# A decoder layer in split fp32: the odd pair of feature blocks goes to the end of the down projection as plain products

## The chip, the cores and the metric

The kernel runs on one core of a Trainium2 chip. The metric is the time of one execution on the device in microseconds. The engines are named as in the profile: PE (TensorE) multiplies matrices into PSUM, DVE (VectorE) and ACT (ScalarE) work element by element, POOL is GpSimd, SP (SyncE) issues most loads. Work from two engines on one piece of data is ordered by semaphores, and each engine executes its own instructions in program order.

## The reference

One layer of a decoder: attention in a window and gated linear attention side by side, an output projection, and a SwiGLU feed-forward part, for a prompt of 1024 tokens and 8 x 8 sample tokens. The change lies in the last product of the feed-forward part:

```python
def swiglu(h, w_gate, w_up, w_down):
    u = jax.nn.silu(jnp.einsum('btd,df->btf', h, w_gate)) * jnp.einsum('btd,df->btf', h, w_up)
    return jnp.einsum('btf,fd->btd', u, w_down)
...
x = x + swiglu(rms_norm(x, norm2[l]), w_gate[l], w_up[l], w_down[l])
```

Here d is 1024 and f is 2816, that is 22 blocks of 128 features. All of it is fp32.

## The kernel before

**Numbers in two halves.** A matrix in fp32 is kept as a rounded part hi and a remainder lo. `split_into` makes both: ACT casts hi (L1230), DVE subtracts to get lo (L1231). A product is three matmuls, hi by hi, hi by lo and lo by hi (`mm3`, L105 to L107), each 128 x 128 by 128 x 512. The sample tokens take two matmuls (`mm2`, L111, L112).

**Seven products instead of eight.** Tokens go in pairs of 128-token tiles (tp = 0 to 3), features in pairs of 128-feature blocks (p = 0 to 10, so NP is 11) and output columns in two halves of 512. For each tp and p there is so a 2 x 2 by 2 x 2 block product. It is done with seven products (numbers m = 1 to 7) of sums of blocks, and the four outputs are sums of the seven results. The seven sums of the left side are made once for all tokens by `tail(p)`: it multiplies the up projection by the activated gate (DVE, L1341), makes sums on POOL (L1351 to L1356), splits each (`put`, tiles named uo in a pool of three) and writes it to device memory `ud[p]` by a DMA issued on ACT's queue (L1348). The down projection reads them back (`load_u`, tiles u, on SP's queue, L1428). The seven sums of the right side come from two raw blocks of w_down (`blocks_W`: load on SP, L83; splits; POOL sums L1375 to L1378).

**The order of the down projection.** `CHUNKS` is (0,), (1, 2), (3, 4) ... (9, 10). For every chunk and tp, seven PSUM tiles (`pd`, eight banks in turn) collect one product for each pair of the chunk, so 21 matmuls in the first chunk and 42 in the others. The results are kept in SBUF as seven tiles Y[tp][m]. The first chunk copies them there, in turn by ACT (L1563) and DVE (L1561), the middle ones add on DVE (L1565). `residual(tp)` adds the residual input to three of the tiles on POOL. In the last chunk `finish` (tp 0 to 2) makes the four outputs from the seven sums while products come in, and for tp 3 `combined` makes sums before the last products and `finish_combined` adds products, in the order of ORDER. Outputs leave by DMAs on ACT's queue. `samples` runs at tp 3 of the first chunk and tp 1 of the others.

PE follows the order in which the program writes matmuls. The other engines' instructions are put in order by a scheduler when the program is built, and no table in the kernel sets it.

Of the kernel before, what the change touches and what calls it, by code (L numbers as in the profile page):

```python
# [37 lines left out]
def hymba_step(ctx: ExitStack, tc: tile.TileContext, x_prompt, x_sample, cache_k, cache_v, state_gla, meta,  # L38
# [1298 lines left out]
    def tail(p, cu, cg):  # L1337
# [11 lines left out]

        put(1, a11), put(2, a12), put(4, a22)  # L1350
# [8 lines left out]
    def blocks_W(pairs):  # L1359
# [12 lines left out]
        put(2, 3, 1)  # L1372
        for raw in raws:
            (b11, b12), (b21, b22) = (halves(r) for r in raw)
            nc.gpsimd.tensor_tensor(b11, b12, b11, op=ALU.subtract)  # L1375
            nc.gpsimd.tensor_tensor(b12, b22, b12, op=ALU.subtract)
            nc.gpsimd.tensor_tensor(b22, b22, b11, op=ALU.subtract)  # L1377
            nc.gpsimd.tensor_tensor(b21, b22, b21, op=ALU.subtract)  # L1378
# [41 lines left out]
    D1, D2 = slice(0, 512), slice(512, 1024)  # L1420

# [8 lines left out]

    def load_u8(p):
# [7 lines left out]
    CHUNKS = [(0,)] + [(p, p + 1) for p in range(1, NP, 2)]  # L1439
# [37 lines left out]
    def finish(tp, x22, m, ps):  # L1477

        y = Y[tp]
        t1, t2 = 2 * tp, 2 * tp + 1  # L1480
        a = y[m]
        if m != 4:
            tt(a, a, ps, op=ALU.add)
        if m == 2:
            ts(a, a, y[1], op=ALU.add)
            nc.scalar.dma_start(yp[rows(t1), D1], a)
        elif m == 7:
            ts(x22, x22, a, op=ALU.add)
            ts(y[4], a, y[4], op=ALU.subtract)
        elif m == 6:  # L1490
            tt(a, a, y[1], op=ALU.add)
            tt(y[1], a, y[5], op=ALU.add)
            ts(x22, x22, y[1], op=ALU.add)
            nc.scalar.dma_start(yp[rows(t2), D2], x22)
            tt(y[3], y[3], y[1], op=ALU.add)
            nc.scalar.dma_start(yp[rows(t1), D2], y[3])
        elif m == 4:
            tt(a, a, ps, op=ALU.subtract)
            tt(a, a, y[6], op=ALU.add)
            nc.scalar.dma_start(yp[rows(t2), D1], a)  # L1500

    def combined(tp, x22):

        y = Y[tp]
        ts(y[2], y[2], y[1], op=ALU.add)
        tt(y[6], y[6], y[1], op=ALU.add)
        tt(y[7], y[7], y[6], op=ALU.add)
        tt(y[1], y[6], y[5], op=ALU.add)
        ts(y[4], y[7], y[4], op=ALU.subtract)
        tt(y[5], y[5], y[7], op=ALU.add)  # L1510
        ts(y[3], y[3], y[1], op=ALU.add)
        ts(y[5], y[5], x22, op=ALU.add)

    def finish_combined(tp, m, ps):
        y = Y[tp]
        t1, t2 = 2 * tp, 2 * tp + 1
        if m == 1:
            nc.scalar.copy(y[6], ps)
            tt(y[2], y[2], ps, op=ALU.add)
        elif m == 2:  # L1520
            tt(y[2], y[2], ps, op=ALU.add)
            nc.scalar.dma_start(yp[rows(t1), D1], y[2])
        elif m == 6:
            tt(y[6], y[6], ps, op=ALU.add)
        elif m == 7:
            tt(y[7], y[6], ps, op=ALU.add)
            ts(y[5], y[5], y[7], op=ALU.add)
            ts(y[4], y[4], y[7], op=ALU.add)
        elif m == 5:
            tt(y[6], y[6], ps, op=ALU.add)  # L1530
            tt(y[5], y[5], ps, op=ALU.add)
            nc.scalar.dma_start(yp[rows(t2), D2], y[5])
            ts(y[3], y[3], y[6], op=ALU.add)
        elif m == 4:
            tt(y[4], y[4], ps, op=ALU.subtract)
            nc.scalar.dma_start(yp[rows(t2), D1], y[4])
        elif m == 3:
            tt(y[3], y[3], ps, op=ALU.add)
            nc.scalar.dma_start(yp[rows(t1), D2], y[3])

    DOWN = (1, 2, 3, 7, 5, 6, 4)
    NC = len(CHUNKS)
    for c, pairs in enumerate(CHUNKS):
        first, last = c == 0, c == NC - 1
        if c:
            W = blocks_W(pairs)
        for tp in range(4):
            U = [load_u(p, tp) for p in pairs]
            if last:
                x22 = xpool2.tile([P, 512], F32, tag="xh", name="x22")  # L1550
                nc.sync.dma_start(x22, x1_rows(2 * tp + 1)[:, D2])
                if tp == 3:
                    combined(tp, x22)
            for j, m in enumerate(ORDER if last and tp == 3 else DOWN):
                ps = pd()
                for i, (u, B) in enumerate(zip(U, W)):
                    mm3(ps, u[m], B[m], i == 0, i == len(pairs) - 1)
                a = Y[tp][m]
                if first:
                    if j % 2:  # L1560
                        nc.vector.tensor_copy(a, ps)  # L1561
                    else:
                        nc.scalar.copy(a, ps)  # L1563
                elif not last:
                    tt(a, a, ps, op=ALU.add)  # L1565
                elif tp == 3:
                    finish_combined(tp, m, ps)
                else:
                    finish(tp, x22, m, ps)
            if c - 1 == tp and not last:  # L1570
                residual(tp)
            if tp == (3 if first else 1):
                samples(pairs, first, last)
# [31 lines left out]
```

## Time and profile before

| | us |
|---|---|
| median of 3 runs (lowest, highest) | 1266.97 (1266.94, 1267.35) |
| profiled execution | 1262.91 |
| its span, first to last instruction | 1260.8 |
| PE busy | 1198.7 (95%) |
| DVE busy | 888.3 (70%) |
| ACT busy | 518.6 (41%) |
| POOL busy | 433.8 (34%) |

Times in the trace count from the start of the span. The down projection runs from about 997.5 us to the end. Engines overlap, so the busy times don't add up to the span. Matmuls are pipelined: a row of one shows 0.39 us, though the next starts 0.23 us later. In a timeline the square bracket at the end of a row is the time in which the engine was idle before it, and what ended it.

### The profile page before, as it was taken

What the parts mean: (1) busy time and instruction counts of PE and PEld (TensorE: products, weight loads), DVE (VectorE), ACT (ScalarE), POOL (GpSimd) and SP (SyncE); (2) the same over time, 40 slices, a digit from 0 to 9 for tenths busy, and PEclk for the clock granted to TensorE, in tenths of its full rate; (3) what the DMA queues carried; (4) which work ended last, traced back from release to release, by engine and by line L of the source; (5) the groups of instructions that cost most, each with busy time, mean ns of one, the idle gap of its engine ahead of it and who ended that gap; (6) DMA issues with size and microseconds to landing.
All of it is one profiled execution on the core that took longest, in us unless ns stands there. A gap on an engine that the chain in (4) does not pass through costs nothing.

```text
span 1260.8 us, 23242 instructions
## 1 busy us (share of the span) xinstructions
PE 1198.7 (95%) x9178; PEld 1062.6 (84%) x9178; DVE 888.3 (70%) x1756; ACT 518.6 (41%) x939; POOL 433.8 (34%) x371
## 2 busy tenths in 40 slices
PE   6999899999999989889999999999999879999995
PEld 6878788778867878889999999999999758888874
DVE  6746886798679767756666666666666675777687
ACT  5634665565565454434333333333333360222110
POOL 6212202131120110225443544354345442534186
PEclk9998999999999989999999999999999979999998
DMA  6723422243312554215524442544354595765555
GB/s 189 231 78 93 119 76 85 53 122 102 101 63 90 182 197 134 84 52 155 167 90 148 150 148 87 175 136 142 97 186 136 186 344 199 280 249 188 224 197 176
DMA packets 146186, 186.31 MB, mean 148 GB/s; under 512 B 15659, under 2 KB 114894, under 8 KB 146062
## 3 DMA queue, kind: packets, MB, share of 16 engines
q1 hardware_dynamic: 94862, 132.40, 32.3%
q10 hardware_dynamic: 49376, 45.56, 11.2%
q0 software_dynamic: 1840, 6.88, 1.6%
q8 instruction: 72, 1.18, 0.4%
q14 instruction: 36, 0.29, 0.1%
HBM read 133.43 MB, written 52.43 MB: 147 GB/s over the span
## 4 chain that ended last, share of the span: by engine, by line
PE 42%; issue 21%; POOL 15%; DVE 14%; ACT 4%; DMA 3%; SPq 0%; POOLq 0%; DVEq 0%; ACTq 0%
PE pd L105 4%; PE pd L106 4%; PE pd L107 4%; POOL raw_wu L1251 2%; ACT hi_wg L1230 2%; POOL raw_wg L1249 1%; PE pf L107 1%; PE gv L105 1%; PE pf L105 1%; PE pf L106 1%; POOL raw_wg L1248 1%; PE gv L107 1%; PE gv L106 1%; PE pw L105 1%; PE pw L106 1%
## 5 line engine op out<-in xcount | busy, mean ns | idle before, releaser
L105 PE MATMUL pd<-hi_wd,u 128*128 128x512 f32 x308 | 121.8, 395 | 13.9 <-ACT y L1563 13.5
L106 PE MATMUL pd<-lo_wd,u 128*128 128x512 f32 x308 | 121.7, 395 | 0.1
L107 PE MATMUL pd<-hi_wd,u 128*128 128x512 f32 x308 | 121.7, 395 | 0.0
L1565 DVE TENSOR_TENSOR y<-y,pd 128x512 f32<-128x512 f32 x112 | 74.7, 683 | 38.3 <-PE pd L107 38.2
L1231 DVE TENSOR_TENSOR uo<-u,uo 128x512 fp32r<-128x512 f32 x77 | 78.2, 1020 | 31.6 <-ACT uo L1230 30.2
L1230 ACT CAST hi_wg<-raw_wg 128x1024 fp32r<-128x1024 f32 (+1 forms) x44 | 41.3, 942 | 139.1 <-PE pf L106 66.0
L1231 DVE TENSOR_TENSOR lo_wu<-raw_wu,hi_wu 128x1024 fp32r<-128x1024 f32 (+1 forms) x44 | 49.2, 1118 | 55.4 <-ACT hi_wu L1230 55.4
L1230 ACT CAST hi_wd<-raw_wd 128x1024 fp32r<-128x1024 f32 x44 | 45.0, 1054 | 99.9 <-PE pd L107 32.2
L1230 ACT CAST uo<-u 128x512 fp32r<-128x512 f32 x77 | 46.7, 620 | 90.8 <-POOL u L1351 44.1
L105 PEld LDWEIGHTS pd<-hi_wd,u 128*128 128x128 f32 x308 | 58.6, 190 | 27.8 <-ACT y L1563 13.9
L1248 POOL TENSOR_TENSOR raw_wg<-raw_wg 128x512 f32<-128x512 f32 x11 | 18.4, 1671 | 160.6 <-DVE lo_wg L1231 135.4
L106 PEld LDWEIGHTS pd<-lo_wd,u 128*128 128x128 f32 x308 | 58.4, 190 | 13.5 <-DVE lo_wd L1231 0.8
L107 PEld LDWEIGHTS pd<-hi_wd,u 128*128 128x128 f32 x308 | 58.5, 190 | 12.7
L1231 DVE TENSOR_TENSOR lo_wg<-raw_wg,hi_wg 128x1024 fp32r<-128x1024 f32 (+1 forms) x44 | 48.9, 1113 | 27.9 <-ACT hi_wg L1230 27.9
L1231 DVE TENSOR_TENSOR lo_wd<-raw_wd,hi_wd 128x1024 fp32r<-128x1024 f32 x44 | 62.8, 1432 | 8.1 <-ACT hi_wd L1230 7.9
L1230 ACT CAST hi_wu<-raw_wu 128x1024 fp32r<-128x1024 f32 (+1 forms) x44 | 41.3, 938 | 55.4 <-POOL raw_wu L1249 28.4
L590 POOL TENSOR_SCALAR sg<-sg 128x512 f32<-128x512 f32 (+1 forms) x9 | 14.0, 1561 | 132.4 <-ACT sg L589 132.3
L106 PE MATMUL pw<-lo_wo,hThi 128*128 128x512 f32 x128 | 51.7, 404 | 4.0 <-DVE lo_wo L100 4.0
L105 PE MATMUL pw<-hi_wo,hThi 128*128 128x512 f32 x128 | 52.9, 413 | 0.3 <-DVE xr L1080 0.3
L107 PE MATMUL pw<-hi_wo,hTlo 128*128 128x512 f32 x128 | 51.3, 400 | 0.0
L1248 POOL TENSOR_TENSOR raw_wu<-raw_wu 128x512 f32<-128x512 f32 x11 | 14.2, 1293 | 89.1 <-DVE lo_wu L1231 89.1
L1377 POOL TENSOR_TENSOR raw_wd<-raw_wd 128x512 f32<-128x512 f32 x11 | 19.9, 1805 | 63.5 <-DVE lo_wd L1231 63.5
(734 smaller groups left out, 4283.0 us busy)
## 6 DMA issues: line engine op xcount, KB each, us to landing
ud<-uo ACTq DMA_DIRECT2D x77, 512.0 KB, 4.2
u<-ud SPq DMA_DIRECT2D x44, 896.0 KB, 6.5
raw_wo<-in_w_o_dram SPq DMA_DIRECT2D x24, 512.0 KB, 4.1
raw_wu<-in_w_up_dram SPq DMA_DIRECT2D x22, 512.0 KB, 4.0
raw_wg<-in_w_gate_dram SPq DMA_DIRECT2D x22, 512.0 KB, 4.3
raw_wd<-in_w_down_dram SPq DMA_DIRECT2D x22, 512.0 KB, 6.4
raw_q<-in_w_in_dram SPq DMA_DIRECT2D x12, 512.0 KB, 3.7
raw_gv<-in_w_in_dram SPq DMA_DIRECT2D x12, 512.0 KB, 3.4
```

Source lines behind the costliest of these rows:

```text
L105: nc.tensor.matmul(ps, lh, rh, start=first, stop=False)
L106: nc.tensor.matmul(ps, lh, rl, start=False, stop=False)
L107: nc.tensor.matmul(ps, ll, rh, start=False, stop=last)
L590: nc.gpsimd.tensor_scalar(s, s, 2.0 ** 60, None, op0=ALU.min)
L1230: nc.scalar.copy(hi, src)
L1231: nc.vector.tensor_tensor(lo, src, hi.bitcast(F32), op=ALU.subtract)
L1248: nc.gpsimd.tensor_tensor(a22, a21, a22, op=ALU.add)
L1249: nc.gpsimd.tensor_tensor(a21, a11, a21, op=ALU.subtract)
L1251: nc.gpsimd.tensor_tensor(a12, a12, a11, op=ALU.subtract)
L1377: nc.gpsimd.tensor_tensor(b22, b22, b11, op=ALU.subtract)
L1565: tt(a, a, ps, op=ALU.add)
```

## The change

The chunks are now (0, 1), (2, 3) ... (8, 9), all of two pairs. In the first one the weights of pair 1 are made right after those of pair 0, and for tp 0 all seven products of pair 0 stand ahead of the seven of pair 1, in seven banks. In chunk (8, 9) each tp ends with `combined(tp)`, which makes the four outputs' sums from the seven. Pair 10 comes last, as plain blocks: four outputs, two products each, added to the sums and written out. So `tail(10)` writes the four blocks themselves, without POOL sums, and `blocks_W` splits the two raw blocks without sums. Its samples run after tp 0 of this phase.

```diff
@@ tail
+        if p == NP - 1:
+            put(1, a11), put(5, a21), put(2, a12), put(4, a22)
+            return
         put(1, a11), put(2, a12), put(4, a22)
@@ blocks_W
-    def blocks_W(pairs):
+    def blocks_W(pairs, plain=False):
...
         put(1, 0, 0)
         put(2, 3, 1)
+        if plain:
+            return W
@@ loads
+    def load_plain(p, tp):
+        u = upool.tile([P, 7, 2, P], F32R, tag="u", name="u")
+        i, j = ORDER.index(5), ORDER.index(4)
+        assert ORDER[0:2] == (1, 2) and j == i + 1
+        nc.sync.dma_start(u[:, 0:2].bitcast(F32), ud[p][tp][:, 0:2])
+        nc.sync.dma_start(u[:, 2:4].bitcast(F32), ud[p][tp][:, i:i + 2])
+        return {m: (u[:, n, 0, :], u[:, n, 1, :]) for n, m in enumerate((1, 2, 5, 4))}
@@ finish, combined and finish_combined go; in their place
+    def combined(tp):
+        y = Y[tp]
+        x22 = xpool2.tile([P, 512], F32, tag="xh", name="x22")
+        nc.sync.dma_start(x22, x1_rows(2 * tp + 1)[:, D2])
         ts(y[2], y[2], y[1], op=ALU.add)
         tt(y[6], y[6], y[1], op=ALU.add)
+        ts(y[4], y[7], y[4], op=ALU.subtract)
         tt(y[7], y[7], y[6], op=ALU.add)
         tt(y[1], y[6], y[5], op=ALU.add)
+        ts(x22, x22, y[7], op=ALU.add)
         ts(y[3], y[3], y[1], op=ALU.add)
+        tt(y[4], y[4], y[6], op=ALU.add)
+        tt(y[5], y[5], x22, op=ALU.add)
@@ the loop
-    CHUNKS = [(0,)] + [(p, p + 1) for p in range(1, NP, 2)]
+    CHUNKS = [(p, p + 1) for p in range(0, NP - 1, 2)]
     for c, pairs in enumerate(CHUNKS):
+        first, last = c == 0, c == len(CHUNKS) - 1
+        W = W + blocks_W((1,)) if first else blocks_W(pairs)
         for tp in range(4):
             U = [load_u(p, tp) for p in pairs]
+            if first and tp == 0:
+                pss = {m: pd() for m in ORDER}
+                for i, (u, B) in enumerate(zip(U, W)):
+                    for m in DOWN:
+                        mm3(pss[m], u[m], B[m], i == 0, i == 1)
+            for j, m in enumerate(DOWN):
+                if first and tp == 0:
+                    ps = pss[m]
+                else:
+                    ps = pd()
+                    for i, (u, B) in enumerate(zip(U, W)):
+                        mm3(ps, u[m], B[m], i == 0, i == 1)
+                a = Y[tp][m]
+                if not first:
+                    tt(a, a, ps, op=ALU.add)
+                elif j % 2:
+                    nc.vector.tensor_copy(a, ps)
+                else:
+                    nc.scalar.copy(a, ps)
+            if (c, tp) in ((1, 0), (2, 1), (3, 2), (3, 3)):
+                residual(tp)
             if last:
+                combined(tp)
+            if tp == (2 if first else 1):
+                samples(pairs, first, False)
+    W = blocks_W((NP - 1,), True)
+    for tp in range(4):
+        u, y = load_plain(NP - 1, tp), Y[tp]
+        B = W[0]
+        for c, (a1, a2), (b1, b2) in ((2, (1, 2), (1, 2)), (4, (5, 4), (1, 2)), (3, (1, 2), (0, 3)), (5, (5, 4), (0, 3))):
+            ps = pd()
+            mm3(ps, u[a1], B[b1], True, False)
+            mm3(ps, u[a2], B[b2], False, True)
+            tt(y[c], y[c], ps, op=ALU.add)
+            nc.scalar.dma_start(yp[rows(2 * tp + (c > 3)), D2 if c in (3, 5) else D1], y[c])
+        if tp == 0:
+            samples((NP - 1,), False, True)
```

**ScalarE at the start of the down projection.** Of the kernel before, from the fifth of the tail's seven operand casts (uo_11451) to the first copy out of PSUM. Tiles uo are the tail's operands on their way to memory, ud10 is that memory; hi_wd_11691 and the two like it are weights of the next chunk.

```order
L1230 CAST uo_11451<-u12_11214 128x4x128
L1230 CAST hi_wd_11691<-raw_wd_11683 128x1024
L1348 DMA ud10_6155<-uo_11446 128x4x256
L1348 DMA ud10_6155<-uo_11451 128x4x256
L1230 CAST uo_11456<-u11_11213 128x4x128
L1230 CAST uo_11460<-u21_11215 128x4x128
L1348 DMA ud10_6155<-uo_11456 128x4x256
L1348 DMA ud10_6155<-uo_11460 128x4x256
L1230 CAST u8hl_11668<-u8_11666 128x2x64
L1230 CAST hi_wd_11695<-raw_wd_11687 128x1024
L1230 CAST hi_wd_11699<-raw_wd_11685 128x1024
L1563 COPY y0_1_11504<-pd_11520 128x512
```

Of the changed kernel, from the last weight cast of pair 0 (hi_wd_11420) to the first copy. The weights 11506, 11510 and 11518 are those of pair 1.

```order
L1230 CAST hi_wd_11420<-raw_wd_11402 128x1024
L1230 CAST hi_wd_11506<-raw_wd_11502 128x1024
L1342 DMA usd10_6166<-u12_11214 128x32
L1230 CAST uo_11436<-u12_11214 128x4x128
L1230 CAST uo_11440<-u21_11215 128x4x128
L1230 CAST uo_11444<-u22_11216 128x4x128
L1348 DMA ud10_6155<-uo_11436 128x4x256
L1348 DMA ud10_6155<-uo_11440 128x4x256
L1348 DMA ud10_6155<-uo_11444 128x4x256
L1230 CAST hi_wd_11510<-raw_wd_11504 128x1024
L1230 CAST hi_wd_11518<-raw_wd_11502 128x1024
L1531 COPY y0_1_11488<-pd_11530 128x512
```

Before, the first copy (L1563) stands behind all seven operand casts, their writes and three weight casts of the next chunk. Now its counterpart (L1531) stands behind four operand casts (uo_11432, the first, is further up), their writes and three casts of weights of pair 1; the fourth of these, hi_wd_11522, is the row after it. The first cast for pair 1 has moved ahead of three operand casts, and the second is behind the three writes.

**TensorE at its eighth and ninth products.** Of the kernel before, the last product of tp 0 and the first two of tp 1; the numbers tell banks (pd), weights and operands apart.

```order
L105 MATMUL pd_11550<-hi_wd_11420,u_11518 128x512
L106 MATMUL pd_11550<-lo_wd_11421,u_11518 128x512
L107 MATMUL pd_11550<-hi_wd_11420,u_11518 128x512
L105 MATMUL pd_11557<-hi_wd_11404,u_11555 128x512
L106 MATMUL pd_11557<-lo_wd_11405,u_11555 128x512
L107 MATMUL pd_11557<-hi_wd_11404,u_11555 128x512
L105 MATMUL pd_11562<-hi_wd_11408,u_11555 128x512
L106 MATMUL pd_11562<-lo_wd_11409,u_11555 128x512
L107 MATMUL pd_11562<-hi_wd_11408,u_11555 128x512
```

Of the changed kernel, the same places.

```order
L105 MATMUL pd_11535<-hi_wd_11420,u_11526 128x512
L106 MATMUL pd_11535<-lo_wd_11421,u_11526 128x512
L107 MATMUL pd_11535<-hi_wd_11420,u_11526 128x512
L105 MATMUL pd_11530<-hi_wd_11506,u_11528 128x512
L106 MATMUL pd_11530<-lo_wd_11507,u_11528 128x512
L107 MATMUL pd_11530<-hi_wd_11506,u_11528 128x512
L105 MATMUL pd_11531<-hi_wd_11510,u_11528 128x512
L106 MATMUL pd_11531<-lo_wd_11511,u_11528 128x512
L107 MATMUL pd_11531<-hi_wd_11510,u_11528 128x512
```

Before, the eighth product takes a new bank, weights that are there, and the operands of tp 1 (u_11555). Now it goes on in the first bank (pd_11530), with weights and operands (u_11528) of pair 1.

**VectorE at the end of the program.** Of the kernel before, from the last four sums of `finish` on; L1519 to L1538 are sums of the last tile out of PSUM.

```order
L1498 TENSOR_TENSOR y_4_11502<-y_4_11502,pd 128x512
L1492 TENSOR_TENSOR y_1_11497<-y_6_11499,y_5_11501 128x512
L1499 TENSOR_TENSOR y_4_11502<-y_4_11502,y_6_11499 128x512
L1495 TENSOR_TENSOR y_3_11503<-y_3_11503,y_1_11497 128x512
L1519 TENSOR_TENSOR y_2_11491<-y_2_11491,pd 128x512
L1521 TENSOR_TENSOR y_2_11491<-y_2_11491,pd 128x512
L1524 TENSOR_TENSOR y_6_11492<-y_6_11492,pd 128x512
L1526 TENSOR_TENSOR y_7_11493<-y_6_11492,pd 128x512
L1530 TENSOR_TENSOR y_6_11492<-y_6_11492,pd 128x512
L1531 TENSOR_TENSOR y_5_11494<-y_5_11494,pd 128x512
L1535 TENSOR_TENSOR y_4_11495<-y_4_11495,pd 128x512
L1538 TENSOR_TENSOR y_3_11496<-y_3_11496,pd 128x512
```

Of the changed kernel, from the first SBUF sum of `combined` for tp 3 on; L1548 adds the plain products.

```order
L1498 TENSOR_TENSOR y_6_11476<-y_6_11476,y_1_11474 128x512
L1527 TENSOR_TENSOR y_4_11479<-y_4_11479,pd 128x512
L1501 TENSOR_TENSOR y_1_11474<-y_6_11476,y_5_11478 128x512
L1500 TENSOR_TENSOR y_7_11477<-y_7_11477,y_6_11476 128x512
L1504 TENSOR_TENSOR y_4_11479<-y_4_11479,y_6_11476 128x512
L1548 TENSOR_TENSOR y_2_11489<-y_2_11489,pd 128x512
L1505 TENSOR_TENSOR y_5_11478<-y_5_11478,x_13129 128x512
L1548 TENSOR_TENSOR y_4_11493<-y_4_11493,pd 128x512
L1548 TENSOR_TENSOR y_3_11494<-y_3_11494,pd 128x512
L1548 TENSOR_TENSOR y_5_11492<-y_5_11492,pd 128x512
```

Before, eight sums out of PSUM stand behind the last sum of `finish`. Now the SBUF sums of the last tile stand ahead of the plain products of all four, and only L1548 (sixteen times) and two sample sums (L1472) come after them.

## Rows read from the trace of the kernel before

**Rows 1.** The page's first part: busy time, share of the span, instructions.

```profile
PE 1198.7 (95%) x9178; PEld 1062.6 (84%) x9178; DVE 888.3 (70%) x1756; ACT 518.6 (41%) x939; POOL 433.8 (34%) x371
```

**Rows 2.** Waits of TensorE from 997 to 1261 us: total, times, longest.

```profile
PE pd L105 <- ACT y L1563: 13.5, 1, 13.5
PE pd L111 <- DVE y L1483: 0.5, 1, 0.5
```

**Rows 3.** Stretches, the last three in the down projection; columns in the first line.

```profile
core 0: us, PE busy (x) PEld busy (x) DVE busy (x) ACT busy (x) POOL busy (x), PEclk, DMA share, GB/s
...
464.00:467.00 3.00, 2.94 (x7) 2.39 (x8) 2.68 (x4) 0.00 (x0) 0.00 (x0) 0.50 0.50 158
...
1017.40:1024.00 6.60, 6.60 (x18) 5.25 (x19) 6.60 (x7) 6.10 (x10) 5.22 (x4) 0.61 0.97 369
1024.00:1211.00 187.00, 186.96 (x817) 153.21 (x816) 131.94 (x173) 42.66 (x54) 74.79 (x47) 1.00 0.64 236
1211.00:1228.35 17.35, 16.73 (x72) 13.10 (x71) 17.28 (x21) 0.04 (x1) 13.47 (x10) 1.00 0.51 181
```

**Rows 4.** TensorE's timeline: start, us, instruction, [idle before, releaser].

```profile
464.06 0.80 PE L106 MATMUL pw<-lo_wo,hThi 128*128 128x512 f32 x1 [3.96 <-DVE lo_wo L100]
...
1003.53 0.39 PE L107 MATMUL pd<-hi_wd,u 128*128 128x512 f32 x1
1017.40 0.79 PE L105 MATMUL pd<-hi_wd,u 128*128 128x512 f32 x1 [13.48 <-ACT y L1563]
...
1018.42 0.63 PE L107 MATMUL pd<-hi_wd,u 128*128 128x512 f32 x1
...
1022.26 0.55 PE L107 MATMUL pd<-hi_wd,u 128*128 128x512 f32 x1
...
1247.35 0.40 PE L107 MATMUL pd<-hi_wd,u 128*128 128x512 f32 x1
```

**Rows 5.** ScalarE's timeline at the start of the down projection.

```profile
998.03 1.05 ACT L1230 CAST hi_wd<-raw_wd 128x1024 fp32r<-128x1024 f32 x1
...
1003.85 0.62 ACT L1230 CAST uo<-u 128x512 fp32r<-128x512 f32 x1 [4.76 <-POOL u L1351]
...
1012.70 0.62 ACT L1230 CAST uo<-u 128x512 fp32r<-128x512 f32 x1 [2.70 <-DMA ud<-uo]
...
1014.87 1.99 ACT L1230 CAST hi_wd<-raw_wd 128x1024 fp32r<-128x1024 f32 x2
1016.77 1.55 ACT L1563 COPY y<-pd 128x512 f32<-128x512 f32 x3
```

**Rows 6.** VectorE's timeline in the last chunk and at the end.

```profile
1225.67 3.66 DVE L1483 TENSOR_TENSOR y<-y,pd 128x512 f32<-128x512 f32 x6
...
1239.74 5.66 DVE L1491 TENSOR_TENSOR y<-y,y 128x512 f32<-128x512 f32 x1
...
1256.75 0.69 DVE L1538 TENSOR_TENSOR y<-y,pd 128x512 f32<-128x512 f32 x1 [0.53 <-POOL y L1533]
```

**Rows 7.** VectorE's timeline at the start of the down projection.

```profile
996.47 2.32 DVE L1231 TENSOR_TENSOR lo_wd<-raw_wd,hi_wd 128x1024 fp32r<-128x1024 f32 x1
998.71 0.68 DVE L1231 TENSOR_TENSOR uo<-u,uo 128x512 fp32r<-128x512 f32 x1
...
1000.54 1.21 DVE L1231 TENSOR_TENSOR lo_wd<-raw_wd,hi_wd 128x1024 fp32r<-128x1024 f32 x1
...
1004.50 1.21 DVE L1231 TENSOR_TENSOR uo<-u,uo 128x512 fp32r<-128x512 f32 x1 [2.11 <-ACT uo L1230]
```

**Rows 8.** GpSimd's timeline there.

```profile
1010.45 1.64 POOL L1375 TENSOR_TENSOR raw_wd<-raw_wd 128x512 f32<-128x512 f32 x1 [2.28 <-DVE lo_wd L1231]
```

**Rows 9.** VectorE's groups from 1200 to 1261 us: busy us, mean ns, idle before.

```profile
L1483 DVE TENSOR_TENSOR y<-y,pd 128x512 f32<-128x512 f32 x18 | 11.2, 675 | 0.0
L1491 DVE TENSOR_TENSOR y<-y,y 128x512 f32<-128x512 f32 x3 | 8.2, 2736 | 0.1
...
L1495 DVE TENSOR_TENSOR y<-y,y 128x512 f32<-128x512 f32 x3 | 5.3, 1773 | 0.0
```

More of the change, by code (lines that the diff above doesn't have):

```diff
@@ L1420, in hymba_step @@
     D1, D2 = slice(0, 512), slice(512, 1024)
+    DOWN = (1, 2, 3, 7, 5, 6, 4)
     def pd():
@@ L1475, in residual @@
         ts(y[4], y[4], x2, op=ALU.subtract)
-    def finish(tp, x22, m, ps):
+    def combined(tp):
         y = Y[tp]
[L1480 to L1500, printed above, removed]
@@ L1502, in combined @@
-    def combined(tp, x22):
-        y = Y[tp]
+        x22 = xpool2.tile([P, 512], F32, tag="xh", name="x22")
+        nc.sync.dma_start(x22, x1_rows(2 * tp + 1)[:, D2])
         ts(y[2], y[2], y[1], op=ALU.add)
         tt(y[6], y[6], y[1], op=ALU.add)
+        ts(y[4], y[7], y[4], op=ALU.subtract)
         tt(y[7], y[7], y[6], op=ALU.add)
         tt(y[1], y[6], y[5], op=ALU.add)
-        ts(y[4], y[7], y[4], op=ALU.subtract)
-        tt(y[5], y[5], y[7], op=ALU.add)
+        ts(x22, x22, y[7], op=ALU.add)
@@ L1511, in combined @@
         ts(y[3], y[3], y[1], op=ALU.add)
[L1512 to L1539, printed above, removed]
@@ L1541, in hymba_step @@
-    DOWN = (1, 2, 3, 7, 5, 6, 4)
-    NC = len(CHUNKS)
+        tt(y[4], y[4], y[6], op=ALU.add)
+        tt(y[5], y[5], x22, op=ALU.add)
+    CHUNKS = [(p, p + 1) for p in range(0, NP - 1, 2)]
     for c, pairs in enumerate(CHUNKS):
-        first, last = c == 0, c == NC - 1
-        if c:
-            W = blocks_W(pairs)
+        first, last = c == 0, c == len(CHUNKS) - 1
+        W = W + blocks_W((1,)) if first else blocks_W(pairs)
         for tp in range(4):
             U = [load_u(p, tp) for p in pairs]
-            if last:
[L1550 to L1573, printed above, removed]
```

## The prediction

> **What bounds the kernel now.** I read the shares of the span first: TensorE is busy 95% of it [rows 1], so a change pays only where TensorE stands still, runs at half clock, or has finished while the rest of the program still runs. Next come the waits of TensorE in the down projection: one of 13.5 us for the copy L1563, and one of 0.5 us for an add of the last chunk [rows 2]. The busy time by stretch shows what an undisturbed matmul costs: 817 in 187.0 us at full clock, 0.2289 us each [rows 3]. The timeline of TensorE then shows the long wait itself: the eighth product's last matmul starts at 1003.53, the ninth product starts at 1017.40, and then the matmuls come 0.427 us apart (nine intervals from 1018.42 to 1022.26) [rows 4], with a granted clock of 0.61 in the stretch [rows 3]: mostly the lower level, 1.2 GHz instead of 2.4. Earlier in the run, after 3.96 us in which TensorE stood still, the clock was at the lower level as well, 0.50 for the next 3 us [rows 3, 4].
>
> The ninth product waits for a bank: there are eight, and the first of them is emptied by the copy L1563 on ScalarE, which begins at 1016.77. ScalarE's own timeline shows what this copy stood behind: four more operand casts of the last up-projection's tail, held by GpSimd's sums (1003.85) and by the landing of earlier writes (1012.70), then casts of down weights [rows 5]. So the stall is a queue on ScalarE, not a lack of data for TensorE. The other loss is the end: the last matmul starts at 1247.35 and is over at 1247.75, and the span ends at 1260.8, 13.05 us in which VectorE and GpSimd work off what they owe [rows 4, 6].
>
> **The sum.** All terms are in the time of the profiled execution: 1262.91 us, of which 2.1 lie outside the span. It is 4.06 below the median of the runs, 1266.97; the change is added to the median.
>
> *More products.* The odd pair takes eight products per tile (token pair) instead of seven, each of three matmuls: 4 x 1 x 3 = 12 more, by 0.2289 us [rows 3]: **+2.75 us**. They are on the engine that bounds, and nothing hides them. The number of sample matmuls stays.
>
> *The start.* Pair 0 needs seven banks, and pair 1 accumulates on the same seven, so no bank is awaited in the first tile; the eighth product instead needs pair 1's weights. The first of them (hi 11506) is cast from a block loaded long before, and stands ahead of the tail's casts on ScalarE. After it ScalarE has three operand casts instead of the six of before, none behind a GpSimd sum; but the issues of the three writes wait for VectorE, and behind these stands the second weight cast, and behind that, on the same queue, half of the copies of tile 0. Step by step: pair 0's last hi cast is over at about 998.8 and hi 11506 at 999.7 (1.0 each [rows 5]); VectorE's two lo parts of 1.21 [rows 7] come after its last work on u, until 1002.4; three small lo parts of 0.68 to 1.21 [rows 7] until 1004.3 to 1006.9, since GpSimd runs its sums for pair 1 beside them. Then a chain through three engines: hi 1.0, lo 1.21 to 2.32 [rows 7], two GpSimd sums at 1.64 [rows 8], hi 1.0, lo 1.21 to 2.32. The last weights are there at 1012.1 to 1015.6 by short and long overlaps. TensorE has done the other products by then and owes two, six matmuls, at 0.427 us while the clock is low. Tile 0 ends at 1013.5 to 1019.5; I take 1016.6, near the middle, as about half of the steps have GpSimd beside VectorE. These are 42 matmuls. Before, 24 are issued up to 1003.53 and 18 from 1017.40 to 1024.0 [rows 3, 4], so the 42nd ends near 1024.0. **-7.4 us (-10.5 to -4.5).** Four of the seven sums are complete before the last weights come, so tile 1 finds banks.
>
> *Pair 1's blocks ahead of the down projection* bring two loads and a cast into the last up-projection, where TensorE bounds; 0, with 0.5 either way.
>
> *The chunk (8,9).* It loses the finishing sums of before: the 0.5 us wait [rows 2] and the other gaps, TensorE being idle 0.62 us of 17.35 in its first half [rows 3]; about -1.0. In their place come, per tile, seven adds from PSUM, five with both operands in SBUF and four on GpSimd. The PSUM adds took 0.675 [rows 9], or 0.61 from one to the next (six in 3.66 [rows 6]): 4.3 us. SBUF sums of this size took 0.68 at the shortest and 1.77 beside GpSimd [rows 7, 9]; I take 1.2 each, between the two, and 1.2 for one wait on GpSimd (a sum there takes 1.64 [rows 8], a part of it over before VectorE asks): 4.3 + 6.0 + 1.2 = 11.5 us per tile. TensorE needs 42 x 0.2289 = 9.6. In four tiles VectorE falls behind by 7.6 us, less 2.4 in the sample products (16 matmuls, 3.7 us, to two adds), plus 2.5 for two lo parts of the last pair: 7.7. Eight banks of 6 x 0.2289 = 1.37 us are a reserve of 11 us, so TensorE hardly waits. With 0.5 us for what I missed: **-0.5 us (-1 to +6).**
>
> *The end.* In the plain phase VectorE has four PSUM adds, 2.7 us with the starts, to TensorE's 24 x 0.2289 = 5.5 us per tile. So it gains 2.8 us a tile, 11 in four, more than the 7.7 it owes. When the last matmul ends, one add and one write are left. Before, from the start of the last add, 1256.75, to the end it took 4.05 us [rows 6]. Against 13.05: **-9.0 us (-8 to -9).** The writes of 16 blocks are spread over 22 us, and only the last one shows.
>
> 2.75 - 7.4 - 0.5 - 9.0 = -14.15: 1248.8 us for a profiled execution, and by the median 1266.97 - 14.15, **about 1253 us**. The bounds together: -18.3 to -3.3.
>
> One row speaks against the chunk term. An SBUF add, L1491, took 5.66 us [rows 6], and the three of this line 2.74 on average, while PSUM adds kept 0.675 [rows 9].
>
> The Trainium skill (SBUF — State Buffer, Who interferes with whom) says why: a VectorE instruction with two SBUF inputs and a GpSimd instruction that reads SBUF share a port pair, the one that issues first keeps it for its whole length, and an add with one SBUF input does not take part. The trace agrees on the PSUM adds; 5.66 us is more than one GpSimd instruction of 1.64 and an add's own 0.68 [rows 7, 8], so a hold can be longer than the rule says. By the rule all four GpSimd instructions of a tile would block an add: 4.3 + 5 x 0.68 + 4 x 1.64 + 1.2 = 15.5 us per tile. That is the bad end of the first rival.
>
> **Rivals.** *VectorE bounds the combining chunk (20%).* If the first SBUF add of a tile takes 2.74, the other four 1.77 [rows 9], and one wait 1.2, a tile costs 4.3 + 2.74 + 7.1 + 1.2 = 15.3 us. The reserve is 11 + 2.4 - 2.5 = 10.9 us, so TensorE waits from 9.6 + 10.9/4 = 12.3 us per tile on: at 15.3 it loses 12, at 13.8, half way, 6. With 6 in place of -0.5 the change is -7.65, or 1259.3 us. For it: the old finishing sums do show such durations. Against: GpSimd then had more to do beside them, and in the new order it stops itself, because its last two instructions of a tile need VectorE sums.
>
> *The start gains nothing (9%).* If the writes' issues on ScalarE are as late as before, since DMA was busy 0.97 right after it [rows 3], the second cast of pair 1 is late too, and tile 0 ends near 1024 as now. Without the 7.4 us: about 1260.2 us. Against: pair 1's blocks are loaded earlier, and the writes are four instead of seven.
>
> *Slower: GpSimd holds the first SBUF add of each tile as in the 5.66 us row (4%).* 4.3 + 5.66 + 7.1 + 1.2 = 18.3 us per tile, 6.0 above 12.3, so 24 us of stall: -13.65 + 24 = +10.4, or 1277 us. It is slower than before from 12.3 + 13.65/4 = 15.7 us per tile on. Against: that needs several GpSimd instructions without a break at each tile, which the one row had from the sample sums and two tiles at once.
>
> *The change moves its losses only (2%).* The start waits as long for weights as for the copy, and at the end the writes of the plain phase queue up so that the last lands 13 us after the last matmul: 2.75 - 0.5, about 1269.
>
> **Numbers.** The forecast has 65%, the rivals 20, 9, 4 and 2%. A measurement of this kernel can tell about 0.2%, 2.5 us, from no change. Only the slower rival, the last one and the bad end of the first come out within that or above: faster 93%, same 3%, slower 4%. The range goes from 1248.5 (start and chunk at their good ends, -18) to 1261, which holds the first two rivals at their prices and leaves out their bad ends.
>
> **What would show it.** In the profile after, TensorE's wait of 13.5 us is gone; in its place stand waits of some us for hi or lo weights of pair 1, with a lower clock after them, and the 43rd matmul comes near 1016.6. In chunk (8,9) TensorE has no wait over 1 us for a bank, and VectorE's SBUF adds average about 1.2. After the last matmul come one add, one write, and about 4 us. Wrong would be: waits for VectorE in the combining chunk, several adds after the last matmul, or a tile 0 that ends past 1020.

## The result, and the profile after

The changed kernel takes 1252.22 us (median of 4 runs, 1249.84 to 1253.08), the kernel before 1266.95 us beside it; the ratio is 0.9887, with a 95% interval of 0.9864 to 0.991. In a later comparison it was 1253.04 against 1265.75 us (0.9904, 0.9885 to 0.9923). So it is faster by 12.7 to 14.7 us; 1253 was forecast, with a range of 1248.5 to 1261.

The profiled execution of the changed kernel takes 1252.41 us, with a span of 1250.6. The two traces can't be compared by the clock time of their rows. The first matmul of the down projection starts at 997.53 before and at 1000.12 after, though the program up to the last tail is the same; over all the traces of this study it starts anywhere from 996.2 to 1004.4. One such difference can be seen: in the trace after, TensorE stands still for 3.3 us near 148 us, in the middle of 128 small matmuls of one kind, and in the trace before it does not. What causes it stays open. I therefore count from that first matmul. The matmuls into the PSUM tiles pd are counted in each trace, and the same four times are read of every kernel (the last column, the down projection, runs from the first matmul to the end of the span):

| us | first to 43rd matmul | 43rd to the end of the last | last matmul to the end | down projection |
|---|---|---|---|---|
| before | 26.50 | 223.71 | 13.03 | 263.2 |
| changed | 18.87 | 225.07 | 6.55 | 250.5 |
| difference | -7.6 | +1.4 | -6.5 | -12.7 |
| forecast | -7.4 | +2.25 | -9.0 | -14.15 |

The waits of TensorE in the down projection (as in [rows 2]): the 13.5 us for the copy are gone, and so is the one for VectorE in the last chunk. In their place stand waits for weights of pair 1.

```profile
PE pd L105 <- ACT hi_wd L1230: 4.7, 2, 4.5
PE pd L106 <- DVE lo_wd L1231: 1.2, 2, 0.8
```

TensorE's timeline (as in [rows 4]): the first matmul, the last of the eighth product (1005.65), the waits, the 43rd matmul (1018.99) and the last.

```profile
1000.12 0.39 PE L105 MATMUL pd<-hi_wd,u 128*128 128x512 f32 x1
...
1005.65 0.40 PE L107 MATMUL pd<-hi_wd,u 128*128 128x512 f32 x1
1010.51 0.79 PE L105 MATMUL pd<-hi_wd,u 128*128 128x512 f32 x1 [4.46 <-ACT hi_wd L1230]
1011.77 0.80 PE L106 MATMUL pd<-lo_wd,u 128*128 128x512 f32 x1 [0.47 <-DVE lo_wd L1231]
1012.37 0.63 PE L107 MATMUL pd<-hi_wd,u 128*128 128x512 f32 x1
...
1016.47 0.51 PE L105 MATMUL pd<-hi_wd,u 128*128 128x512 f32 x1 [0.28 <-ACT hi_wd L1230]
1017.73 0.50 PE L106 MATMUL pd<-lo_wd,u 128*128 128x512 f32 x1 [0.76 <-DVE lo_wd L1231]
...
1018.99 0.39 PE L105 MATMUL pd<-hi_wd,u 128*128 128x512 f32 x1
...
1243.66 0.40 PE L107 MATMUL pd<-hi_wd,u 128*128 128x512 f32 x1
```

The eighth product goes on without a stop, the ninth waits 4.46 us for its hi weights and 0.47 us for the lo part, and the matmuls behind them come 0.42 us apart. The granted clock in stretches (columns as in [rows 3]) was 0.71 and 0.59 of full speed from 1006 to 1016, a mixture of its two levels (1.2 and 2.4 GHz), and full from 1018.4 to 1225, with TensorE busy all the time there:

```profile
1006.00:1012.00 6.00, 1.07 (x3) 0.52 (x3) 4.48 (x4) 2.47 (x3) 2.46 (x3) 0.71 0.92 301
1012.00:1016.00 4.00, 4.00 (x11) 2.96 (x11) 2.01 (x3) 0.63 (x1) 3.26 (x2) 0.59 1.10 385
1018.40:1175.00 156.60, 156.60 (x686) 128.29 (x685) 104.79 (x136) 41.29 (x55) 57.33 (x39) 1.00 0.67 248
1175.00:1225.00 50.00, 50.00 (x220) 41.05 (x219) 43.45 (x57) 4.11 (x4) 30.95 (x20) 1.00 0.52 190
```

ScalarE's timeline (as in [rows 5]) shows why the weights came late. The three operand casts are over at 1004.8. Then the queue issues the three writes, each when VectorE's lo part is ready, and only at 1009.41 comes the second weight cast (the x2 row holds it and the third); the last one, at 1015.37, waits for GpSimd's sum.

```profile
1003.15 1.66 ACT L1230 CAST uo<-u 128x512 fp32r<-128x512 f32 x3 [0.83 <-DVE u L1341]
1005.65 3.72 ACTq L1348 DMA_DIRECT2D ud<-uo  x3
1009.41 1.99 ACT L1230 CAST hi_wd<-raw_wd 128x1024 fp32r<-128x1024 f32 x2 [4.60 <-DVE uo L1231]
...
1015.37 1.05 ACT L1230 CAST hi_wd<-raw_wd 128x1024 fp32r<-128x1024 f32 x1 [3.48 <-POOL raw_wd L1384]
```

From 1175 us on, VectorE's groups (as in [rows 9]) show 32 sums out of PSUM (28 of chunk (8,9), four of the chunk before it) and 16 of the plain phase at 0.68 us, as before, and 20 SBUF sums (the last five rows):

```profile
L1527 DVE TENSOR_TENSOR y<-y,pd 128x512 f32<-128x512 f32 x32 | 20.2, 677 | 0.0
L1548 DVE TENSOR_TENSOR y<-y,pd 128x512 f32<-128x512 f32 x16 | 10.3, 681 | 3.4 <-PE pd L107 3.4
...
L1500 DVE TENSOR_TENSOR y<-y,y 128x512 f32<-128x512 f32 x4 | 7.1, 1774 | 3.6 <-POOL y L1499 3.6
L1498 DVE TENSOR_TENSOR y<-y,y 128x512 f32<-128x512 f32 x4 | 2.8, 693 | 0.1
L1505 DVE TENSOR_TENSOR y<-y,x 128x512 f32<-128x512 f32 x4 | 2.8, 692 | 2.4 <-POOL x L1502 2.4
L1501 DVE TENSOR_TENSOR y<-y,y 128x512 f32<-128x512 f32 x4 | 2.7, 685 | 0.0
L1504 DVE TENSOR_TENSOR y<-y,y 128x512 f32<-128x512 f32 x4 | 2.7, 678 | 0.0
```

Their mean is (7.1 + 2.8 + 2.8 + 2.7 + 2.7) / 20 = 0.905 us. Where one is longer, the two timelines lie side by side, VectorE's first and GpSimd's second:

```profile
1202.63 0.69 DVE L1501 TENSOR_TENSOR y<-y,y 128x512 f32<-128x512 f32 x1
1204.50 1.77 DVE L1500 TENSOR_TENSOR y<-y,y 128x512 f32<-128x512 f32 x1 [1.19 <-POOL y L1499]
```

```profile
1202.79 1.68 POOL L1499 TENSOR_TENSOR y<-y,y 128x512 f32<-128x512 f32 x1 [2.42 <-DVE y L1527]
1204.43 1.29 POOL L1503 TENSOR_TENSOR y<-y,y 128x512 f32<-128x512 f32 x1
```

L1500 starts 0.07 us after GpSimd's L1503 and ends 0.55 us after it: it was held for the rest of one GpSimd instruction. L1501 had started first and ran its usual 0.69, and GpSimd's L1499 took 1.68 instead of 1.3. In these rows the rule of the Trainium skill (SBUF — State Buffer, Who interferes with whom) holds as it is written: the first to start keeps the ports, and the other waits for one instruction. It does not hold in the 5.66 us row of the kernel before [rows 6]: that sum outlasted four GpSimd instructions in a row, none longer than 2.40 us.

The end is the part that came out worse than forecast. The last matmul ends at 1244.06, the last sum is ready at 1244.78:

```profile
1244.09 0.69 DVE L1548 TENSOR_TENSOR y<-y,pd 128x512 f32<-128x512 f32 x1 [0.69 <-PE pd L107]
```

But ScalarE's queue is not: its first row here is the copy for the sample outputs, and the write at 1238.66 is theirs.

```profile
1233.73 1.05 ACT L1477 COPY y8lo<-y 64x1024 f32<-64x1024 f32 x1 [42.19 <-DVE y L1472]
1234.27 0.34 ACTq L1549 DMA_DIRECT2D out_dram<-y  x1
1238.66 0.55 ACTq L1480 DMA_DIRECT2D out_dram<-y8lo  x1
1239.30 7.68 ACTq L1549 DMA_DIRECT2D out_dram<-y  x11
```

That write needs GpSimd's second sample sum:

```profile
1236.22 2.41 POOL L1479 TENSOR_TENSOR y8lo<-y8lo,x 64x1024 f32<-64x1024 f32 x1
```

It ends at 1238.63. Until then the queue stands, with finished output blocks behind that write, and then issues eleven output writes in 7.68 us, 0.70 each. The last is issued from 1246.40 to 1246.98, 1.6 us after its sum was ready, among others that have still to land.

### The profile page after: what moved, and what is told of

Same layout as the page of the kernel before. It is cut to its first block, busy times and chain, and to the rows that moved or that the text cites. A ratio compares the mean times of both kernels' runs of the same rounds, so it can differ in the third digit from the quotient of the medians.

```text
span 1250.6 us, 23186 instructions
## 1 busy us (share of the span) xinstructions
PE 1202.3 (96%) x9190; PEld 1065.3 (85%) x9190; DVE 873.1 (70%) x1742; ACT 514.7 (41%) x933; POOL 415.2 (33%) x360
## 4 chain that ended last, share of the span: by engine, by line
PE 47%; issue 21%; POOL 14%; DVE 12%; ACT 4%; DMA 1%; SPq 0%; POOLq 0%; ACTq 0%; DVEq 0%
PE pd L106 6%; PE pd L105 5%; PE pd L107 5%; POOL raw_wu L1251 2%; ACT hi_wg L1230 2%; POOL raw_wg L1249 1%; PE pf L107 1%; PE gv L105 1%; PE pf L105 1%; PE pf L106 1%; POOL raw_wg L1248 1%; PE gv L107 1%; PE gv L106 1%; DVE uo L1231 1%; PE pw L105 1%
## 5 line engine op out<-in xcount | busy, mean ns | idle before, releaser
L105 PE MATMUL pd<-hi_wd,u 128*128 128x512 f32 x312 | 123.4, 395 | 4.7 <-ACT hi_wd L1230 4.7
L107 PE MATMUL pd<-hi_wd,u 128*128 128x512 f32 x312 | 122.7, 393 | 0.0
L1394 ACT ACTIVATE g<-g 128x544 f32<-128x544 f32 x44 | 28.9, 656 | 23.7 <-DVE g L1284 19.8
```

Of the source, the lines that this page charges most:

```text
L105: nc.tensor.matmul(ps, lh, rh, start=first, stop=False)
L107: nc.tensor.matmul(ps, ll, rh, start=False, stop=last)
L1394: nc.scalar.activation(a, a, AF.Silu)
```

## The experiments

**What the start's gain comes from.** Theory A: from pair 1 accumulating in pair 0's banks. Theory B: from the shorter tail. Two further kernels, with the one before and the changed one, give a table of two by two.

Seven operands written, new order in the first tile:

```diff
             put(1, a11), put(5, a21), put(2, a12), put(4, a22)
+            ts(a22, a21, a22, op=ALU.add)
+            ts(a21, a11, a21, op=ALU.subtract)
+            ts(a11, a22, a11, op=ALU.subtract)
+            put(7, a21)
+            ts(a12, a12, a11, op=ALU.subtract)
+            put(6, a11), put(3, a12)
             return
```

> The changed kernel, but the last tail again makes its four GpSimd sums and writes seven operands (the three extra ones are read by nobody). The start of the down projection is measured as the time from its first matmul to the 43rd: 26.5 us in the kernel before, 18.9 in the changed one. Theory A (the gain comes from pair 1 accumulating in pair 0's banks, so that TensorE waits for weights and not for the copy): most of it stays; the second weight cast stands behind two more operand casts and GpSimd's sums, 2 to 4 us later, so 21 to 23 us, and the whole 2 to 4 us above the changed kernel. Theory B (the gain comes from the shorter tail): the start goes back to about 26, +7.

Four operands written, old order (the first tile is written as all others, one product for each pair of the chunk):

```diff
-    CHUNKS = [(p, p + 1) for p in range(0, NP - 1, 2)]
+    CHUNKS = [(0,), (9,)] + [(p, p + 1) for p in range(1, NP - 2, 2)]
...
-        W = W + blocks_W((1,)) if first else blocks_W(pairs)
+        if c:
+            W = blocks_W(pairs)
...
```

> The changed kernel, but the down projection starts as before with pair 0 alone, seven banks copied out per tile; pair 9 is a single chunk right behind it, then (1,2) to (7,8) and the plain pair 10. The last tail has four writes, as changed. Theory A: TensorE waits for the first copy as in the kernel before; the start (to the 43rd matmul) takes 24 to 26.5 us and the whole is 5 to 8 us above the changed kernel. Theory B: the copy now stands behind three operand casts and their write issues only, so it comes about 9.5 us after the first matmul; the wait is 4 us, with 2 us of low clock, and the start takes 16 us: 3 us less than the changed kernel. Both: the end as in the changed kernel, 6.5 us after the last matmul.

| first to 43rd matmul, us | seven operands | four operands |
|---|---|---|
| old order (pair 0 alone) | 26.50 (before) | 16.27 |
| new order (pairs 0 and 1) | 27.57 | 18.87 (changed) |

Each figure is one trace. Where a start is repeated in other runs of this study, the changed one takes 18.87 to 19.14, the new order with seven operands 27.57 and 27.78, the old order with four 16.27 and 15.11; behind nearly the same wait (3.65 and 3.49 us) the last two have eleven and six matmul distances of 0.43 us.

Medians on one chip: seven operands in the new order 1261.25 (10 runs, ratio 0.9947, 0.9927 to 0.9966), four in the old order 1251.42 (4 runs, 0.9874, 0.9841 to 0.9906), before 1267.84. Theory A falls: the new order by itself gives nothing. With four operands it costs 2.6 to 3.8 us up to the 43rd matmul, and the old order loses 1.1 of that again later, at two short waits for lo weights in its third chunk; the 1.1 us with seven operands are within the spread of the old order's two traces. The shorter tail gives 8.7 us in the new order, where it is the only edit. The 10.2 us of the old order are not the tail's alone: the chunk behind pair 0 is there pair 9 instead of pairs 1 and 2, and in the kernel before three weight casts of that chunk (3.0 us) stand ahead of the first copy. ScalarE's timeline of the kernel with seven operands in the new order, from the three issues on, shows where the time goes:

```profile
1007.73 3.71 ACTq L1348 DMA_DIRECT2D ud<-uo  x3
1017.96 0.62 ACT L1230 CAST uo<-u 128x512 fp32r<-128x512 f32 x1 [11.07 <-DMA ud<-uo]
1019.33 0.62 ACT L1230 CAST uo<-u 128x512 fp32r<-128x512 f32 x1 [0.75 <-DMA ud<-uo]
...
1019.86 1.04 ACT L1230 CAST hi_wd<-raw_wd 128x1024 fp32r<-128x1024 f32 x1
```

The next operand cast stands 11.07 us, in the end for the landing of an earlier write, since the pool of operand tiles has three buffers; the second weight cast of pair 1 (1019.86) is behind it. With four operands in all, the three late ones just fit, because the first was written long before (its write landed at 992.84 in the trace after). But the cast also needs a sum of GpSimd's, and the first of these to be split ends at 1013.7: with more buffers it would still have stood about 7 of the 11 us. In the kernel before, too, ScalarE waited for both, 4.76 us for GpSimd and then 2.70 for a landing [rows 5]. No run has more buffers with seven operands, so how the gain divides between GpSimd's sums, the writes and the casts stays open. In the old order the copies come right behind the three issues, and the wait for a bank is short:

```profile
1001.70 3.38 ACTq L1348 DMA_DIRECT2D ud<-uo  x3
1005.12 2.55 ACT L1524 COPY y<-pd 128x512 f32<-128x512 f32 x5 [4.26 <-DVE y L1522]
```

```profile
PE pd L105 <- ACT y L1524: 3.6, 1, 3.6
```

**The order within the first tile.** Pair 1's product follows pair 0's in each bank:

```diff
-                for i, (u, B) in enumerate(zip(U, W)):
-                    for m in DOWN:
+                for m in DOWN:
+                    for i, (u, B) in enumerate(zip(U, W)):
                         mm3(pss[m], u[m], B[m], i == 0, i == 1)
```

> The changed kernel, but in the first tile each product of pair 0 is followed by that of pair 1 in the same bank, as in all later tiles, instead of all of pair 0 first. Theory A (putting pair 0 first fills the wait for pair 1's weights): TensorE stops after three products instead of eight, and as the last weights come no earlier, the 43rd matmul comes 1 to 4 us later than 18.9 us after the first. Theory B says nothing of this edit; if the order does not matter, 18.9 us.

First to 43rd matmul 20.27 us (one run, 1250.73 us in all): 1.4 us more, against a spread of 0.3 in the starts of the changed kernel. TensorE stands 2.6 us before its fourth matmul, for operands of pair 1, and 2.9 before its tenth, for the second weight cast. Putting pair 0 first does help, given that the first chunk has two pairs.

**The writes ahead of the second weight cast.**

```diff
-            nc.scalar.dma_start(ud[p][:, :, ORDER.index(m)]...
+            (nc.sync if p == NP - 1 and m != 1 else nc.scalar).dma_start(ud[p][:, :, ORDER.index(m)]...
```

> The changed kernel with one edit: the last three operand writes of the last tail are issued on SyncE instead of ScalarE, so that the second weight cast of pair 1 no longer stands behind them. My theory: ScalarE casts it about 4 us earlier, VectorE's lo part follows its three small ones about 1.5 us earlier, and so do GpSimd's two sums and the last weights: the start takes 17 us instead of 18.9. Rival: the operand loads of tile 1, now behind these writes on SyncE's queue, come late and TensorE waits for them: 19 us or more.

17.29 us, 1.6 less, and TensorE's wait is now for the lo part, not for the hi cast:

```profile
PE pd L106 <- DVE lo_wd L1231: 4.3, 2, 3.9
```

The median, 1253.48 (4 runs, ratio 0.9889, 0.9855 to 0.9923), can't show so little beside the spread of the first 1000 us. The step is as I had put it: the writes hold the cast, which now comes 4.60 us after the first matmul instead of 9.29, and VectorE's three lo parts are next in line.

**The end.** One edit, the sample outputs' write goes to another queue:

```diff
-            nc.scalar.dma_start(ys, y8)
+            nc.sync.dma_start(ys, y8)
```

> The changed kernel with one edit: the write of the sample outputs is issued on SyncE instead of ScalarE. In the changed kernel ScalarE's queue stands at this write until GpSimd's second sample sum (4 us), and eleven output writes follow it one after the other at 0.70 us, the last of them 2.2 us after its sum was ready. My theory: the end after the last matmul falls from 6.5 to about 4.1 us, so 2.4 us in all. Rival: the writes are held by their issue or by DMA rate all the same, and the end stays at 6 to 6.5 us.

The end falls from 6.55 to 4.00 us after the last matmul, and the down projection from 250.5 to 248.0; median 1249.83 (4 runs, ratio 0.9862, 0.9831 to 0.9893). ScalarE's queue then issues twelve writes over 10.84 us without a backlog at the end (the last is issued at 1242.66, 0.03 us after its sum), and the last sum starts at 1241.94 with 1245.9 the end of the span: 4.0 us, what the last add and write took before [rows 6].

```profile
1231.61 1.05 ACT L1477 COPY y8lo<-y 64x1024 f32<-64x1024 f32 x1 [42.78 <-DVE y L1472]
1232.16 10.84 ACTq L1549 DMA_DIRECT2D out_dram<-y  x12
```

```profile
1241.94 0.69 DVE L1548 TENSOR_TENSOR y<-y,pd 128x512 f32<-128x512 f32 x1 [0.69 <-PE pd L107]
```

This settles the end: the 2.5 us came from the place of that one write in the queue.

**What the plain phase is for.** The kernel before with the new start, so that pair 10 stands alone at the end with its seven products and the old finishing sums (the edits that go with the new chunks are left out here):

```diff
-    CHUNKS = [(0,)] + [(p, p + 1) for p in range(1, NP, 2)]
+    CHUNKS = [(p, p + 1) for p in range(0, NP - 1, 2)] + [(NP - 1,)]
...
```

> The kernel before with the new start: chunks (0,1) to (8,9), then pair 10 alone with the seven products and the finishing sums of before, seven operands written. It tells what the plain phase does for the end. A tile of pair 10 has 21 matmuls, 4.8 us, while VectorE's finishing takes 9 to 11 us. If VectorE's work then bounds the last chunk: 16 to 20 us of waiting less a reserve of 5 to 8, and an end of 10 us or more after the last matmul; from the 43rd matmul to the end 245 us or more, against 236.7 in the kernel before and 231.6 in the changed one. If the end depends only on what follows the last matmul: about 237.

43rd matmul to the end: 246.8 us, against 236.7 before and 231.6 after the change (one run, 1276.44 us). It writes seven operands, and its start takes 27.78 us, so only the time from the 43rd matmul on is compared. The end comes 16.5 us after the last matmul. VectorE's last rows are the sums that it owes, some of them held by GpSimd for 3 us:

```profile
1253.82 3.06 DVE L1508 TENSOR_TENSOR y<-y,y 128x512 f32<-128x512 f32 x1
1256.81 2.99 DVE L1491 TENSOR_TENSOR y<-y,y 128x512 f32<-128x512 f32 x1
...
1270.62 0.69 DVE L1538 TENSOR_TENSOR y<-y,pd 128x512 f32<-128x512 f32 x1 [0.53 <-POOL y L1533]
```

So a chunk of one pair doesn't carry the old finishing sums without a long end; in the plain phase, with one PSUM sum for each six matmuls, VectorE catches up.

**VectorE's reserve in the combining chunk.**

```diff
                 combined(tp)
+                for k in range(8):
+                    tt(Y[tp][6], Y[tp][6], Y[tp][6], op=ALU.max)
```

> The changed kernel with eight more VectorE instructions with two SBUF operands behind the sums of each tile in chunk (8,9) (a maximum of a finished tile with itself, which changes no value). It measures the reserve of eight banks by which VectorE may be late there. VectorE's tiles take 10.4 to 11.5 us now and would take 15.3 to 16.5. With a reserve of about 11 us, as the prediction worked it out, TensorE waits for about 10 us in all, and the down projection takes 260 instead of 250.5 us. If VectorE bounded from the first tile on, without a reserve: 271 us. If more is hidden (the plain phase gives time back): 250.5 to 253 us.

The down projection took 270.7 us (one run, 1274.4 us in all): 20 more, not 10. TensorE's waits for VectorE are 13.3 us:

```profile
PE pd L105 <- DVE y L1550: 6.8, 1, 6.8
PE pd L105 <- DVE y L1472: 5.6, 1, 5.6
PE pd L105 <- DVE y L1527: 0.9, 1, 0.9
```

VectorE's tiles, from one L1498 to the next, took 16.6, 17.5 and 14.8 us, 16.3 on average and so within what I had expected, with sums of up to 1.78 us. Most of the other 5.4 us before the last matmul follow the waits of 5.6 and 6.8 us: behind each, TensorE's matmuls are 0.43 us apart for a while, its clock mostly at the lower level (granted 0.70 and 0.50 of full speed in the stretches that follow). The end grew by 1.5 us. That there is a reserve holds, since the first wait comes in the third tile; the price of a wait has to include the clock behind it.

**Versions after that.** Old start, and both sets of writes on SyncE:

> The kernel with the old start (pair 0 alone, then pair 9, four operand writes), the sample outputs' write on SyncE, and the last tail's three operand writes on SyncE as well. If the start is set by what stands ahead of the first copies on ScalarE and VectorE (theory B), then with the write issues gone the first copy comes about 5 us after the first matmul and the bank wait of 3.6 us shrinks to 1 us or less, with no time at the low clock: 43rd matmul after 10 to 13 us instead of 16.3, end 4.0 us after the last matmul, down projection 241 to 243 us, and a median near 1244 us. Rival: the loads of tile 3 and pair 9, now behind the writes on SyncE, or VectorE's copies behind its three lo parts hold TensorE instead, and the start stays at 15 to 16 us.

First to 43rd matmul 13.62 us, 2.7 less than with the old start alone, but the 169th comes 47.39 us after the first instead of 45.11. Median 1252.08 (6 runs, ratio 0.9883, 0.9864 to 0.9903). The down projection takes 249.0 us, not the 241 to 243 expected. The rival was right about the cause, though not about the start, which it put at 15 to 16 us: after five copies ScalarE stands 8.13 us, because the next instruction in its queue casts sample operands whose load was behind the writes on SyncE.

```profile
1003.48 2.52 ACT L1524 COPY y<-pd 128x512 f32<-128x512 f32 x5
1014.14 0.30 ACT L1230 CAST u8hl<-u 128x128 fp32r<-128x128 f32 x1 [8.13 <-DMA u<-usd]
1014.35 0.58 ACT L1524 COPY y<-pd 128x512 f32<-128x512 f32 x1
```

Old start, and only the sample outputs' write on SyncE:

> The old start with four operand writes (as in the run with that name) and, as its one further edit, the sample outputs' write on SyncE. The two gains are at both ends of the down projection and should add: start 16.3 us, end 4.0 us after the last matmul, down projection 246.5 us against 250.5 in the changed kernel and 263.2 before; about 4 us below the changed kernel on the same chip. Rival: the gain at the start is taken back by the chunk of pair 9 alone, whose VectorE adds run at half the products per add; then no more than 2.5 us.

15.11 us of start, 4.00 of end, down projection 245.3 us; median 1250.55 (5 runs, 1248.36 to 1251.18; ratio 0.9874, 0.9853 to 0.9896). The gains add. That the start is 1.2 us shorter than with the old start alone lies mostly in a shorter time at the low clock, for which no edit accounts. The last tail's late writes on GpSimd's queue instead:

> As the run before, with the last tail's three operand writes issued on GpSimd instead of ScalarE. On SyncE they held the loads behind them; GpSimd has three sums of pair 9 behind them, needed ten us later. My theory: the first copy comes about 5 us after the first matmul, the wait for a bank falls to 2 us or less, no load is late: start 11 to 14 us, 169th matmul 40 to 43 us after the first instead of 45.1, down projection 241 to 244 us. Rival: an issue on GpSimd is slow or holds VectorE's lo parts, pair 9's sums come late, and the 169th matmul is at 45 us or later.

13.59 us of start, but the 169th matmul at 44.53, against 43.95 without the edit; down projection 246.0, median 1251.17 (6 runs, ratio 0.9886, 0.9867 to 0.9905). No gain, where 40 to 43 us and 241 to 244 us were expected: TensorE waits twice for 1.8 us instead of once for 3.5. The changed kernel beside these two:

> The changed kernel as it is, for comparison with the two others on the same chip: 18.9 us of start, 6.5 us of end, a down projection of 250.5 us, and a median 14 to 15 us below the kernel before.

19.14, 6.56 and 250.8 us; median 1253.04 (6 runs, 1251.65 to 1257.04). All five runs of the version with the old start and the moved write are below all six of the changed kernel; the medians differ by 2.5 us, the down projections in the traces by 5.5. The 3 us between the two must lie ahead of the down projection, where the traces differ by up to 8, and are not explained. In this comparison it beats both kernels.

## Why the prediction was right, and where it was not

*The total* was right, and less well founded than it looks. The terms gave -14.15, the trace -12.7 in the down projection; the median of the first comparison, -14.7, has the spread of the first 1000 us in it, and the second comparison gave -12.7.

*The start* was right in size, and its chain was right step by step. Forecast -7.4, measured -7.6. The chain from the lo parts over the writes' issues to the second hi cast, GpSimd's sums and the last weights came as worked out, shifted by the 2.6 us by which the whole down projection began later: the last lo part was due at 1012.1 to 1015.6, that is 1014.7 to 1018.2, and ended at 1017.7. That the sum came within 0.2 us is in part luck. The last weights came 1.2 us later than the middle of their range, and the matmuls behind them took 1.3 us instead of the 2.6 that six at 0.427 us would: five were left, at a clock that was full again (granted 1.00 from 1016 to 1019). The late bound, 1019.5, is not the chain's either; 1015.6 and those 2.6 us give 1018.2. What the prediction did not do is to price the two parts of the edit apart. Read from its own words, "no bank is awaited", the new order would get the credit; the table of four kernels gives it to the shorter tail.

*More products* (+2.75) *and the chunk* (-0.5): +2.25 forecast, +1.4 measured. The chunk term was mis-sized, -0.5 for -1.4: it held 0.5 us for things missed, and there were none (the 982 matmuls from the 43rd on take 225.07 us, and 982 x 0.2289 is 224.8), and the gaps of before came to 1.4 us instead of 1.0. VectorE's work there was off as well, without a price: the SBUF sums took 0.905 on average, not 1.2, the waits for GpSimd came to 1.8 us per tile instead of 1.2, and TensorE waited for none of it. A tile of VectorE without sample sums and lo parts took 10.4 us against 11.5 forecast; two with them, which the forecast had counted apart, took 11.3 and 11.5.

*Pair 1's blocks ahead of the down projection* (0, with 0.5 either way) can't be checked: the time up to the first matmul varies by 8 us over the traces, and no run has this edit alone.

*The end* failed in one sentence, "The writes of 16 blocks are spread over 22 us, and only the last one shows". They were not spread: the sample write stood in the middle of the same queue. Forecast -9.0, with bounds of -8 to -9, measured -6.5; with that write elsewhere it is -9.0. The diff itself places the samples after the first tile of the plain phase, and their write is issued on the queue of the output blocks.

*The rivals.* VectorE did not bound the chunk, the first SBUF sum of a tile was never held (L1498, 0.69 each), and GpSimd's run did break after two instructions. The changed kernel, with tiles of up to 11.5 us and no wait, and the run with eight more sums, with 16.3 on average and 13.3 us of waits, put the point where TensorE begins to wait between the two; the 12.3 of the prediction is not tested more closely.

## What to carry to other kernels

When two engines seem to block each other, list what stands ahead of the waited-for instruction on its own queue, and count the buffers that these need: here seven operands through three buffers, with sums of another engine among them, kept the queue from the copies, and a new order of the banks did not help. An output write that needs a slow chain is better kept off a queue with writes that are ready: here that cost 2.5 us. When a change has two parts, price them apart, since one of them may be paying for the other.

## What was not expected of the hardware

A wait costs more than its length: behind waits of 4.5 to 13.5 us, six to ten matmuls came 0.43 us apart instead of 0.23, the clock at its lower level. The length of the wait does not tell how many: behind 3.65 us in one run there were eleven, behind 3.49 in another six. In the version with the writes on GpSimd a wait of 1.84 us was followed by four matmuls 0.23 to 0.34 us apart and then by eight at 0.39 to 0.43; a wait of 1.76 us twelve us later was followed by none.

A VectorE sum of two SBUF operands can be held by more than one GpSimd instruction: 5.66 us in the kernel before, and 3.06 and 2.99 in the run with the old end, against 1.77 where GpSimd stopped after two instructions.
